# Attention kernel without softmax: the last two groups' stores go over the GpSimd queue instead of the SP queue

## The chip, the cores and the metric

The kernel runs on one core of a Trainium2 chip. A core has engines that work side by side: TensorE (PE, matrix products), VectorE (DVE), ScalarE (ACT), GpSimd (POOL) and SyncE (SP). Transfers between the device memory and the on-chip memory are done by 16 DMA engines; an instruction on an engine's queue issues a transfer and does not wait for it. The metric is the device time of one execution in microseconds (us), as the median of several runs.

## The reference

For each of 8 x 12 heads with 512 rows of 64 numbers (all float32):

```python
Q_feat = np.maximum(0, Q) + 1
K_feat = np.maximum(0, K) + 1
KV = np.einsum('bhkd,bhkv->bhdv', K_feat, V)
K_sum = np.sum(K_feat, axis=2)
numerator = np.einsum('bhqd,bhdv->bhqv', Q_feat, KV)
denominator = np.einsum('bhqd,bhd->bhq', Q_feat, K_sum)
return (numerator / (denominator[:, :, :, None] + 1e-10)).astype(np.float32)
```

Q, K, V and the output have 12.6 MB each.

## The kernel before

The rows of all heads are put into 12 groups (`NG = 12`, g = 0 to 11); a group has 1 MiB of each tensor. Two groups with the same `g // 2` share the tiles of the loads and the output tile `o_sb`, of which there are three (`OUT_BUFS = 3`).

For each group the kernel does these steps: `k_features` (L137, VectorE, maximum and addition on K), `v_blocks` (L153 and L155, V into a tile of blocks, three quarters on VectorE and one on ScalarE), `keys_values` (L171, TensorE; its result is copied by ScalarE, L181 and L182), `q_features`, `transposes` (L192, TensorE; copied at L195), `out_matmuls` (L205, TensorE) and `norms` (L222 reciprocal and L223 multiply, VectorE), which writes `o_sb`. A group has two halves h, and each half four such VectorE instructions. `store(g)` sends the group's part of `o_sb` to the output.

The order of the instructions on each engine is the order in which they are written (`tc.manual_schedule()`), and the semaphore waits between the engines follow from the data. In the main loop over g the K, V and Q loads of later groups are issued on the GpSimd queue (L106, L112), and the store of group g - 3 (`LAG = 3`) at the end of the body, on GpSimd as well. Only the very first K load goes over SP (L93). The last two groups are written out by hand after the loop; the program ends with the stores of groups 8 to 11:

```python
        output(last - 1)
        output(last)
        for g in range(last - LAG, NG):
            store(g)
```

`store` sends groups 0 to 9 over GpSimd (L126, 1 MiB each), group 10 over SP (L129, 1 MiB) and group 11 over SP in two pieces, one for each half (L132, 512 KiB each). After the last instruction the launch code (its lines in the trace are L327) closes the program: SP waits for all transfers, each engine drains (an instruction DRAIN on its queue), and the engines meet in two rounds of semaphores, in which GpSimd collects the others' signals and releases them.

Of the kernel before, what the change touches and what calls it, by code (L numbers as in the profile page):

```python
# [19 lines left out]
def kernel(  # L20
# [19 lines left out]
    nc = tc.nc  # L40
# [8 lines left out]
    NP = 4  # L49
    NG = NPAIR // NP  # L50
# [37 lines left out]
    outs = {}  # L88
# [33 lines left out]
    def store(g):  # L122
        s = g // 2
        o_to = o_dram[:, 2 * NP * s : 2 * NP * s + 2 * NP]
        if g < NG - 2:
            nc.gpsimd.dma_start(out=o_to[:, g % 2 : 2 * NP : 2], in_=outs[s][:, g % 2 : 2 * NP : 2])  # L126
            return
        if g == NG - 2:
            nc.sync.dma_start(out=o_to[:, 0 : 2 * NP : 2], in_=outs[s][:, 0 : 2 * NP : 2])  # L129
            return  # L130
        for h in range(2):
            nc.sync.dma_start(  # L132
                out=o_to[:, 2 * h + g % 2 : 2 * NP : NP], in_=outs[s][:, 2 * h + g % 2 : 2 * NP : NP]
            )

# [111 lines left out]
    with tc.manual_schedule():  # L247
# [17 lines left out]
        for g in range(last - 1):  # L265
            if g % 2:
                transposes(g - 1)
            k_features(g)
            v_blocks(g)
            if g >= 2:  # L270
                output(g - 2)
            if g % 2:
                transposes(g)
            else:
                q_features(g)
                q_features(g + 1)
            keys_values(g)
            if g % 2 and g // 2 + 2 < NG // 2:
                load_pair(g // 2 + 2)
            if g >= LAG:  # L280
                store(g - LAG)
# [5 lines left out]
        v_blocks(last)  # L287
        keys_values(last - 1)
        store(last - 1 - LAG)
        q_features(last - 1)  # L290
        q_features(last)
# [8 lines left out]
        for g in range(last - LAG, NG):  # L300
            store(g)
# [30 lines left out]
```

## Time and profile before

| | |
|---|---|
| time, median of 3 runs | 127.17 us (127.16 to 127.29) |
| span of the profiled execution, first to last instruction | 125.0 us |
| busy: VectorE, TensorE, ScalarE, GpSimd | 89.1, 62.7, 59.6, 26.1 us |
| moved by DMA queue q0 (GpSimd's) and q1 (SP's) | 28.84 and 3.15 MB |
| last multiply (L223) | 117.18 to 117.87 us |
| issues of stores 8 and 9 on GpSimd | 98.50 and 110.19 us |
| issues of store 10 and of the two pieces of store 11 on SP | 114.54, 116.22 and 117.90 us |

Apart from its span, no time of the profiled execution by itself is listed; the median lies 2.2 us above the span, which is time before the first and after the last instruction of the program. Times in the text are in us from the start of the span. POOLq and SPq are the instruction queues of GpSimd and SP: their semaphore, drain and DMA instructions stand there and don't count as busy time.

### The profile page before, as it was taken

The page shows a single profiled execution, that of the slowest core. Times are in us where ns is not written, and L with a number is a line of the kernel's source. Part 1 is how long each engine was busy: PE and PEld are TensorE (multiplying, and loading weights), DVE is VectorE, ACT ScalarE, POOL GpSimd, SP SyncE. Part 2 cuts the span into 40 slices and gives each one's busy share as a digit, 9 for nine tenths or more (in the row PEclk, how much of TensorE's full clock was granted, in tenths as well). Part 3 has the DMA queues.
Part 4 walks back from the last instruction along what each step waited for, and adds up shares of the span by engine and source line. Part 5 has one row for each costly group of instructions (what it writes and reads, how often), then busy time and mean ns, then how long its engine had stood idle before and what let it go on. Part 6 is the DMA issues. An engine that isn't in the chain of part 4 may idle for free.

```text
span 125.0 us, 2348 instructions
## 1 busy us (share of the span) xinstructions
PE 62.7 (50%) x960; PEld 51.3 (41%) x960; DVE 89.1 (71%) x190; ACT 59.6 (48%) x86; POOL 26.1 (21%) x52
## 2 busy tenths in 40 slices
PE   0004945200593837539684691079494457775300
PEld 0003735200482827428573491057393255663100
DVE  4895444206999899997999930799948699969700
ACT  7532289306029781956539462601992295450000
POOL 6991023000001630233302430302020200020000
PEclk9999999955589999995999679756999558997555
DMA  3999999999999999999999999999999999999992
GB/s 94 329 220 207 208 195 208 209 213 214 210 210 212 219 214 207 211 214 220 227 404 328 213 212 214 215 347 391 228 211 216 216 267 417 420 410 417 408 403 103
DMA packets 11803, 32.13 MB, mean 257 GB/s; under 512 B 528, under 2 KB 528, under 8 KB 11792
## 3 DMA queue, kind: packets, MB, share of 16 engines
q0 software_dynamic: 10448, 28.84, 97.2%
q1 hardware_dynamic: 1344, 3.15, 6.7%
q8 instruction: 7, 0.11, 0.3%
q14 instruction: 4, 0.03, 0.1%
HBM read 37.75 MB, written 12.58 MB: 403 GB/s over the span
## 4 chain that ended last, share of the span: by engine, by line
DMA 53%; DVE 23%; PE 8%; ACT 6%; issue 3%; POOL 2%; POOLq 0%
DMA v_raw<-in_V_dram 53%; DVE v_all L155 8%; DVE o_sb L223 8%; PE kva_ps L171 5%; ACT v_all L153 3%; DVE qf L137 2%; PE qt_ps L192 2%; DVE recip L222 2%; ACT qt L195 2%; DVE kf L137 1%; DVE qt L195 1%; ACT kva_all L181 1%; POOL v_raw L106 1%; POOL k_raw L106 1%; PE o_ps L205 1%
## 5 line engine op out<-in xcount | busy, mean ns | idle before, releaser
L205 PE MATMUL o_ps<-kva_all,qt 128*64 128x130 bf16 x384 | 20.5, 244 | 36.9 <-DVE recip L222 27.3
L171 PE MATMUL kva_ps<-v_all,kf 128*64 128x260 bf16 x384 | 30.1, 322 | 15.5 <-DVE v_all L155 15.3
L155 DVE COPY v_all<-v_raw 32x2048 bf16<-32x2048 bf16 x36 | 25.8, 717 | 13.5 <-DMA v_raw<-in_V_dram 13.1
L223 DVE TENSOR_TENSOR o_sb<-o_ps,recip 128x512 f32<-128x512 f32 x48 | 33.2, 692 | 1.7
L171 PEld LDWEIGHTS <-kf 128*64 128x64 bf16 x384 | 24.7, 131 | 18.8 <-DVE v_all L155 15.7
L205 PEld LDWEIGHTS <-qt 128*64 128x64 bf16 x384 | 14.3, 120 | 42.1 <-issue 27.3
L153 ACT COPY v_all<-v_raw 32x2048 bf16<-32x2048 bf16 x12 | 22.6, 1893 | 17.1 <-DMA v_raw<-in_V_dram 16.9
L195 ACT COPY qt<-qt_ps 128x1024 bf16<-128x1024 bf16 x23 | 22.2, 1015 | 6.7 <-PE qt_ps L192 6.4
L181 ACT CAST kva_all<-kva_ps 64x256 bf16<-64x256 f32 x24 | 8.9, 371 | 27.7 <-PE kva_ps L171 27.5
L126 POOL DMA_DIRECT2D out_dram<-o_sb x10 | 8.6, 863 | 35.9 <-DVE o_sb L223 27.5
L192 PE MATMUL qt_ps<-identity,qf 128*128 128x128 bf16 x192 | 14.9, 236 | 1.8 <-ACT qt L195 1.2
L192 PEld LDWEIGHTS <-qf 128*128 128x128 bf16 x192 | 12.5, 106 | 4.5 <-issue 2.5
L137 DVE TENSOR_SCALAR kf<-k_raw 128x1024 bf16<-128x1024 bf16 x22 | 8.5, 429 | 7.8 <-DMA k_raw<-in_K_dram 7.8
L106 POOL DMA_DIRECT2D k_raw<-in_K_dram x6 | 4.9, 811 | 35.2 <-DVE kf L137 35.2
L222 DVE RECIPROCAL recip<-o_ps 128x8 f32<-128x8 f32 x48 | 9.6, 200 | 1.4 <-PE o_ps L205 1.2
L137 DVE TENSOR_SCALAR qf<-q_raw 128x1024 bf16<-128x1024 bf16 x24 | 8.8, 432 | 2.1 <-DMA q_raw<-in_Q_dram 2.1
L106 POOL DMA_DIRECT2D v_raw<-in_V_dram x7 | 5.4, 766 | 13.1 <-ACT v_all L153 9.3
L240 DVE MEMSET v_all<- 128x2600 f32 x2 | 4.5, 2225 | 1.1 <-issue 1.1
L112 POOL DMA_DIRECT2D q_raw<-in_Q_dram x6 | 4.2, 708 | 0.0
L182 ACT CAST kva_all<-kva_ps 64x4 bf16<-64x4 f32 x24 | 4.1, 169 | 0.0
L241 ACT COPY v_all<-zero 128x1560 f32<-128x1560 f32 x2 | 2.9, 1488 | 0.0
L261 POOL MEMSET kva_all<- 128x130 bf16 x16 | 2.4, 201 | 0.0
(13 smaller groups left out, 5.7 us busy)
## 6 DMA issues: line engine op xcount, KB each, us to landing
out_dram<-o_sb POOLq DMA_DIRECT2D x10, 1024.0 KB, 25.9
q_raw<-in_Q_dram POOLq DMA_DIRECT2D x6, 1024.0 KB, 26.2
k_raw<-in_K_dram POOLq DMA_DIRECT2D x5, 1024.0 KB, 21.9
v_raw<-in_V_dram POOLq DMA_DIRECT2D x5, 1024.0 KB, 23.2
k_first<-in_K_dram SPq DMA_DIRECT2D x1, 1024.0 KB, 4.8
v_raw<-in_V_dram POOLq DMA_DIRECT2D x2, 512.0 KB, 10.7
out_dram<-o_sb SPq DMA_DIRECT2D x1, 1024.0 KB, 7.0
out_dram<-o_sb SPq DMA_DIRECT2D x2, 512.0 KB, 6.4
```

The costliest lines, as they stand in the source:

```text
L106: nc.gpsimd.dma_start(out=bufs[x, s][:, ms], in_=drams[x][:, of])
L126: nc.gpsimd.dma_start(out=o_to[:, g % 2 : 2 * NP : 2], in_=outs[s][:, g % 2 : 2 * NP : 2])
L137: nc.vector.tensor_scalar(out=dst, in0=src, scalar1=1.0, scalar2=1.0, op0=ALU.add, op1=ALU.max)
L153: nc.scalar.copy(out=v_all[ps, g % 2, :, :, b * D : b * D + D], in_=v_raw[ps])
L155: nc.vector.tensor_copy(out=v_all[ps, g % 2, :, :, b * D : b * D + D], in_=v_raw[ps])
L171: nc.tensor.matmul(kva_ps[64 * n : 64 * n + 64], lhsT=kf[:, c, n, :], rhs=v_all[:, g % 2, n, c, :], start=(c == 0), stop=(c == C2 - 1),)
L181: nc.scalar.copy(out=kva[ps, :, n, 0:D], in_=kva_ps[ps, 0 : 4 * D].rearrange("p (b d) -> p b d", b=4))
L192: nc.tensor.transpose(qt_ps[:, c, r], qf[:, r, 2 * half + c, :, :], identity)
L195: copy(out=qts[g // 2][:, lo : lo + 2], in_=qt_ps.rearrange("p c r q -> p c q r"))
L205: nc.tensor.matmul(ops[c // 4][64 * j : 64 * j + 64, c // 2 % 2, (c % 2) * W : (c % 2) * W + W], lhsT=qt[:, c, q : q + 16, :], rhs=kva[:, ...
L222: nc.vector.reciprocal(out=recip, in_=cells[:, :, :, :, D:D1])
L223: nc.vector.tensor_tensor(out=o_sb[:, 2 * h + g % 2 : 2 * NP : NP, 4 * i : 4 * i + 4].rearrange("p n (b c) d -> p b c n d", b=2), in0=cell ...
```

## The change

The stores of groups 10 and 11 are issued on the GpSimd queue, like those of all other groups: group 10 in one piece, by the branch that groups 0 to 9 take, and group 11 in the same two pieces as before. SP issues no store any more. Nothing else differs.

```diff
     def store(g):
         s = g // 2
         o_to = o_dram[:, 2 * NP * s : 2 * NP * s + 2 * NP]
-        if g < NG - 2:
+        if g < NG - 1:
             nc.gpsimd.dma_start(out=o_to[:, g % 2 : 2 * NP : 2], in_=outs[s][:, g % 2 : 2 * NP : 2])
             return
-        if g == NG - 2:
-            nc.sync.dma_start(out=o_to[:, 0 : 2 * NP : 2], in_=outs[s][:, 0 : 2 * NP : 2])
-            return
         for h in range(2):
-            nc.sync.dma_start(
+            nc.gpsimd.dma_start(
                 out=o_to[:, 2 * h + g % 2 : 2 * NP : NP], in_=outs[s][:, 2 * h + g % 2 : 2 * NP : NP]
             )
```

## The prediction

> **What bounds the kernel now.** I read the page's slices first: what limits the end?
>
> ```profile
> DMA  3999999999999999999999999999999999999992
> GB/s 94 329 220 207 208 195 208 209 213 214 210 210 212 219 214 207 211 214 220 227 404 328 213 212 214 215 347 391 228 211 216 216 267 417 420 410 417 408 403 103
> ```
>
> The 16 DMA engines are full from the second slice to the last but one; from slice 34 (103 us) on they move stores only, at 403 to 420 GB/s. Next, the windows of the last stretch (columns: window, length, busy time of PE, PEld, DVE, ACT and POOL, granted clock, DMA share, GB/s):
>
> ```profile
> 118.00:119.00 1.00, 0.00 (x0) 0.00 (x0) 0.00 (x0) 0.00 (x0) 0.00 (x0) 0.50 1.05 408
> 121.00:122.00 1.00, 0.00 (x0) 0.00 (x0) 0.00 (x0) 0.00 (x0) 0.00 (x0) 0.50 0.97 375
> 122.00:123.00 1.00, 0.00 (x0) 0.00 (x0) 0.00 (x0) 0.00 (x0) 0.00 (x0) 0.50 0.61 238
> 123.00:124.00 1.00, 0.00 (x0) 0.00 (x0) 0.00 (x0) 0.00 (x0) 0.00 (x0) 0.50 0.09 35
> ```
>
> After the last multiply (117.87 us) nothing computes; 6 us of transfers follow. The engines do not finish together: the first run dry about 122, the last at 124. Third, the DMA queues (packets, MB, time of their packets as a share of 16 engines) in the window 116 to 116.5 and then in 119 to 121; no other queue moved anything in either:
>
> ```profile
> q0 software_dynamic: 53, 0.21, 102.5%
> ```
>
> ```profile
> q1 hardware_dynamic: 419, 0.82, 105.3%
> ```
>
> q0 is POOL's queue, q1 is SP's. SP issued group 10's store at 114.54, yet up to 116.5 only q0 moves data. From 116.5 the engines change over one after the other (88.6% against 12.1% in 116 to 117, 2.1% against 105% in 118.5 to 119). So the SP stores lie behind POOL's stores 8 and 9 anyway, as if they stood in one line. Fourth, the landings: POOL's store 9 alone, then SP's last piece alone (duration, start, issue to landing):
>
> ```profile
> L126 POOL DMA_DIRECT2D out_dram<-o_sb x1: 752/752/752, 110.2 to 110.2; - x1
> ...
> DMA to landing us min/median/max: 9.1/9.1/9.1
> ```
>
> ```profile
> L132 SPq DMA_DIRECT2D out_dram<-o_sb x1: 372/372/372, 117.9 to 117.9; - x1
> ...
> DMA to landing us min/median/max: 6.2/6.2/6.2
> ```
>
> Store 9 has landed at 110.2 + 9.1 = 119.3; the last piece at 117.9 + 6.2 = 124.1. Last, what lies between that landing and the end of the span: the closing instructions of POOL, one view of 109 to 115 us and one of 124.2 to 124.35, and SP's waits:
>
> ```profile
> L327 POOLq DRAIN  x1: 10325/10325/10325, 110.2 to 110.2; - x1
> ```
>
> ```profile
> L327 POOLq EVENT_SEMAPHORE  x2: 17/17/17, 124.2 to 124.3; - x2
> ```
>
> ```profile
> SPq L327 <- DMA out_dram<-o_sb: 5.4, 4, 2.0
> ```
>
> SP waits for each store's landing, then drains; POOL's EVENT_SEMAPHORE collects the engines at 124.24, releases them, and two short drains and a second round end the span at 125.0. The row I build on is the first: POOL's closing DRAIN stands behind store 9's issue and lasts to 110.2 + 10.3 = 120.5. POOL's last issue was over at 110.9, so it is not POOL's own work that it waits out; its end lies 1.2 us behind the landing of POOL's last DMA (119.3). Now it is finished 3.7 us before anyone needs POOL.
>
> **The change part by part.**
>
> Removed: one SP issue (0.38 us) and two (0.37 us). SP has nothing else at that time; taking them away frees 0, and the transfers still wait for the same multiplies.
>
> Added: three issues on POOL, 0.75 us each as store 9 (the POOL row gives 0.75 to 1.13 for a store). The first is ready when group 10's last multiply ends (114.51), the others at 116.19 and 117.87, so POOL issues at about 114.54, 116.22 and 117.90: 1.7 us apart, each done before the next is due. Nothing else is queued on POOL between store 9 and its DRAIN.
>
> A wait that could come in: a POOL store waits for the landing of the POOL DMA eight issues before it. The waits view shows it ("POOL out_dram L126 <- DMA k_raw" 2.0 us: store 4 waited to 74.0 for the K load eight issues before). For the three new ones these are the last V load, the last Q load and store 4: landed at 99.1, 103.9 (71.32 + 32.6) and 106.5 (74.02 + 32.5). All lie before 114.5: 0.
>
> Supply: are the transfers in the queue before an engine runs dry? No row shows POOL's delay from issue to first packet on an idle queue. Bounds: 0.75 us (the issue) and 3.5 us (the first V load was issued at 1.30, its first packets come in the window 4.5 to 5.0, when the engines leave the first K load). I take 0.75, and 3.5 changes nothing: group 10's store then starts at 118.0, while the engines leave store 9 between 116.5 and 118.9; early ones idle up to 1.5 us, but they have 2 us in hand at the end (dry at 122 against 124). The last piece would be there by 121.4; the last engine gets to it at about 122.8 (landing of the piece before it, 116.2 + 6.6). The cover is this backlog; without it, up to 3.5 us less SP's own delay would stand at the end.
>
> A rule speaks against the change here. The row: store 3's issue took 1.13 us against 0.75. The Trainium skill, SBUF — State Buffer, "SBUF: two separate sides", says that GpSimd cannot write a DMA's descriptors while VectorE runs an operation in a two-port mode; its section "A bandwidth-pool intuition that's wrong (but worth ruling out)" gives 620 ns growing to about 3100. No issue here is that long; by 3.1 us the last piece would be queued at 121.0, still ahead of 122.8, and the sum would stay.
>
> Pace: 2 MB move from q1 to q0. q0 alone moves 417 GB/s in 106 to 110, q1 alone 409 in 119 to 121: 5.03 against 5.13 us for 2.1 MB, a gain of 0.1 us at best. By landings, stores 5 to 8 landed at 109.0, 111.5, 114.0 and 116.5 (79.3 + 29.7 up to 98.5 + 18.0), 2.5 us per MB; 3 MB more from 116.5 give 124.0 to 124.1, which is where SP's last piece lands now. So I take 0, and keep -0.1. The last landing stays at 124.1.
>
> The close: POOL's DRAIN now stands behind the issue at 117.9. If it follows the last POOL landing as it does now, it ends at 124.1 + 1.2 = 125.3, and POOL's EVENT_SEMAPHORE moves from 124.24 to 125.33 (0.03 us behind the drain, as behind the later drain at 124.41 + 0.10). SP's waits end as now, so POOL is the last to arrive. Cost 1.1 us. Everything after it (125.0 - 124.24 = 0.7 us) moves along: span 126.1. Bounds of the 1.2 us: it is one reading; at 0.2 us the cost would be 0.1, at 1.9 (half as much again) 1.7.
>
> Here a second rule differs from the trace. The row: 10.3 us of DRAIN, 9.6 of them after POOL's issue had ended. The Trainium skill, PSUM — Partial Sum Buffer, "Engine vs sequencer instructions", says that a drain waits until the engine is fully idle and speaks of no transfers; read so, the drain would end with the last issue, about 118.7, and the change would cost 0. The row decides.
>
> Sum: 0 (SP) + 0 (POOL's issues) + 0 (supply) + 0 (pace) + 1.1 (drain). The profiled execution has a span of 125.0 us; the median of the three runs is 127.17, so 2.2 us lie outside the span and stay. 125.0 + 1.1 + 2.2 = 128.3; from the median, 127.17 + 1.09 = 128.26.
>
> **The rivals.**
>
> No cost (not slower): the drain has no tie to the landing, or its 1.2 us shrink when the queue empties. Then the end is the last landing as now: 127.07 to 127.2. It decides from the point where the drain ends less than 0.4 us after the landing (0.17 brings it to 124.24, 0.25 more is the bound of what can be told). For it: one reading only. Against: POOL had no work in these 9.6 us, and of the events nearby only store 9's landing comes close before the end.
>
> A fixed drain: it lasts 9.6 us behind POOL's last issue whatever the transfers do. Last issue over at 118.65, drain to 128.2, event 4.0 us later than now: 131.2. Against: three other drains of POOL, with no transfer open, last 0.05 to 0.2 us.
>
> A starved tail: POOL's issues are slow beside VectorE, or its queue starts later than 3.5 us, and engines run dry for 0.5 to 1.5 us besides the drain: 128.8 to 129.8. The rows against it are those of the supply.
>
> **How the numbers follow.** Drain behind the landing 0.80 (127.7 to 128.9), no cost 0.10, fixed drain 0.03, starved tail 0.04, a gain of more than 0.25 us for a reason I don't see 0.03. A difference under 0.2% (0.25 us) can't be told from none: slower 0.87, same 0.10, faster 0.03. Range 127.5 to 129.0: it leaves out no cost, fixed drain, the unseen gain and most of the starved tail, together 0.19.
>
> **What would show it.** The profile after should have a POOL DRAIN from 117.9 to about 125.3, ending 1.2 us behind the last landing; that landing at 124.1; no q1 packets after the first K load; and POOL's event right behind its drain, with SP waiting for it. A last landing off 124.1 by over 0.3 us breaks supply or pace; a drain ending by 124.2 breaks the forecast.

## The result, and the profile after

The changed kernel takes 128.28 us (median of 6 runs, 127.73 to 128.44) where the kernel before took 126.98 us in the same series (6 runs, 126.41 to 127.29): a ratio of 1.0103, with an interval of 1.0078 to 1.0128. The change costs 1.3 us. (The six runs before include the three that the prediction started from, 127.16 to 127.29; the three new ones took 126.41 to 126.80.) The profiled execution took 128.1 us, with a span of 126.3 us against 125.0 before.

Line numbers behind `store` are three lower in the changed kernel: the multiply is L220, and the closing instructions are L324. First the transfers of the tail, in the page's slices (now 3.16 us each) and in the queues between 120 and 122 us (packets, MB, share of 16 engines):

```profile
DMA  3999999999999999999999999999999999999980
GB/s 80 331 220 206 210 191 211 212 217 215 207 211 212 219 212 210 209 213 217 261 412 281 208 213 215 218 384 359 217 210 219 215 323 416 422 412 412 414 348 9
```

```profile
q0 software_dynamic: 221, 0.82, 100.2%
```

The stores move through q0 alone and at the same pace (412 to 422 GB/s in the full slices; 0.82 MB in these 2 us, as q1 had in its two). What is new is the last slice: 9 GB/s where there had been 103. The program goes on after its transfers are over. The last piece's issue and landing, POOL's closing drain with the event behind it (a window around 125.6), and SP's waits show why:

```profile
L129 POOL DMA_DIRECT2D out_dram<-o_sb x1: 719/719/719, 118.9 to 118.9; - x1
...
DMA to landing us min/median/max: 5.3/5.3/5.3
```

```profile
L324 POOLq DRAIN  x1: 6722/6722/6722, 118.9 to 118.9; - x1
L324 POOLq EVENT_SEMAPHORE  x1: 17/17/17, 125.6 to 125.6; - x1
```

```profile
SPq L324 <- DMA out_dram<-o_sb: 122.9, 5, 115.6
SPq L324 <- PEq L324: 1.8, 2, 1.3
```

The last piece has landed at 118.88 + 5.3 = 124.2. The drain lasts to 118.86 + 6.72 = 125.58, and only then, at 125.62, does POOL collect the engines. Before, that event stood at 124.24. The last wait of SP, 1.3 us, is new. Before, it was 0.5 us:

```profile
SPq L327 <- PEq L327: 0.6, 2, 0.5
```

In the view after, the wait is put down to PE's queue, but PE had drained by 117.7; what came last was POOL's drain. A releaser's name in such a line is a guess that the times have to confirm.

### The profile page after: what moved, and what is told of

Its sections match the earlier page's. It is cut to its first block, busy times and chain, and to the rows that moved or that the text cites. A ratio compares the mean times of both kernels' runs of the same rounds, so it can differ in the third digit from the quotient of the medians.

```text
span 126.3 us, 2349 instructions
## 1 busy us (share of the span) xinstructions
PE 66.7 (53%) x960; PEld 53.9 (43%) x960; DVE 89.6 (71%) x190; ACT 59.6 (47%) x86; POOL 28.4 (22%) x55
## 3 DMA queue, kind: packets, MB, share of 16 engines
q0 software_dynamic: 11008, 30.94, 100.3%
## 4 chain that ended last, share of the span: by engine, by line
DMA 52%; issue 24%; POOL 6%; DVE 5%; ACT 4%; PE 3%; POOLq 1%
DMA v_raw<-in_V_dram 30%; DMA out_dram<-o_sb 22%; DVE v_all L152 3%; PE kva_ps L168 2%; POOL out_dram L126 2%; ACT qt L192 2%; ACT v_all L150 2%; POOL v_raw L106 1%; DVE o_sb L220 1%; POOL q_raw L112 1%; POOLq L324 1%; ACT kva_all L178 1%; POOL k_raw L106 1%; POOL out_dram L129 1%; PE o_ps L202 1%
## 5 line engine op out<-in xcount | busy, mean ns | idle before, releaser
L168 PE MATMUL kva_ps<-v_all,kf 128*64 128x260 bf16 x384 | 35.2, 359 | 14.8 <-DVE v_all L152 14.8
L202 PE MATMUL o_ps<-kva_all,qt 128*64 128x130 bf16 x384 | 20.0, 240 | 35.3 <-DVE recip L219 24.3
L168 PEld LDWEIGHTS <-kf 128*64 128x64 bf16 x384 | 28.0, 148 | 19.6 <-DVE v_all L152 15.2
L220 DVE TENSOR_TENSOR o_sb<-o_ps,recip 128x512 f32<-128x512 f32 x48 | 33.2, 692 | 1.7
L126 POOL DMA_DIRECT2D out_dram<-o_sb x11 | 9.4, 853 | 39.2 <-DVE o_sb L220 27.8
```

The lines of the kernel that those rows point to most:

```text
L168: nc.tensor.matmul(kva_ps[64 * n : 64 * n + 64], lhsT=kf[:, c, n, :], rhs=v_all[:, g % 2, n, c, :], start=(c == 0), stop=(c == C2 - 1),)
L202: nc.tensor.matmul(ops[c // 4][64 * j : 64 * j + 64, c // 2 % 2, (c % 2) * W : (c % 2) * W + W], lhsT=qt[:, c, q : q + 16, :], rhs=kva[:, ...
L220: nc.vector.tensor_tensor(out=o_sb[:, 2 * h + g % 2 : 2 * NP : NP, 4 * i : 4 * i + 4].rearrange("p n (b c) d -> p b c n d", b=2), in0=cell ...
```

## The experiments

Two theories stood at the start. **A:** POOL's closing DRAIN ends a certain distance behind the landing of POOL's own last DMA, and only what of that reaches beyond SP's last wait costs time. **B:** every byte that is moved from SP's queue to POOL's costs something by itself, through late supply or a slower pace. A third, **C**, was that any move away from SP costs. Four kernels put the three issues on different queues. (The experiments' kernels choose the queue in a variable, so their line numbers are off by one or a few: the closing instructions are L324 to L328, the issues of the last pieces L129 to L133.)

**The first two on POOL, the last piece on SP.** Against the changed kernel:

```diff
-        for h in range(2):
-            nc.gpsimd.dma_start(
+        for h, queue in enumerate((nc.gpsimd, nc.sync)):
+            queue.dma_start(
```

> Store 10 and the first piece of store 11 on POOL, the last piece on SP. Theory A (the closing drain of POOL ends 1.2 to 1.35 us behind the landing of POOL's own last DMA, and costs only what of that lies behind SP's last wait): POOL's last landing about 122.9, drain to 124.1 to 124.3, SP's last landing 124.1; the close is where it was, cost 0 to 0.1 us, time within 0.2% of before. Theory B (the 1.5 MB of 2 MB moved to POOL cost by themselves, through supply or pace): about three quarters of the change's 1.3 us, so +1.0 us.

Measured: ratio 1.0035 (1.0016 to 1.0055), +0.44 us. The interval, 0.2 to 0.7 us, holds neither A's 0 to 0.1 nor B's 1.0. The profile says why:

```profile
L130 POOL DMA_DIRECT2D out_dram<-o_sb x1: 707/707/707, 116.6 to 116.6; - x1
...
DMA to landing us min/median/max: 6.8/6.8/6.8
```

```profile
L325 POOLq DRAIN  x1: 8097/8097/8097, 116.6 to 116.6; - x1
```

POOL's last piece lands at 123.3 and not at 122.9, because SP's piece, issued at 118.0, is served beside it: SP's first packet starts at 119.30, POOL's last one at 122.93. Behind store 10's last landing (121.62) the last landings of the two pieces follow 1.72 and 0.80 us apart, where in the changed kernel they follow 1.25 apart. The drain ends 1.31 us behind that landing, at 124.65, and POOL's event comes 0.56 us behind the last of all landings, against 0.17 before. The difference, 0.39 us, lies within the interval of the cost. The theory's distance was right; the landing that I had put into it was wrong.

**Only store 10 on POOL.** Against the kernel before:

```diff
-        if g < NG - 2:
+        if g < NG - 1:
...
-        if g == NG - 2:
-            nc.sync.dma_start(out=o_to[:, 0 : 2 * NP : 2], in_=outs[s][:, 0 : 2 * NP : 2])
-            return
```

> Only store 10 on POOL, both pieces of store 11 on SP. Theory A: POOL's last landing about 121.6, drain to 122.9, over 1.2 us before SP's last landing of 124.1: cost 0. Theory B: half of the 2 MB is moved, +0.65 us.

Measured: ratio 0.9998 (0.9974 to 1.0021). Half of the bytes are moved and nothing is lost; B's +0.65 us is out.

```profile
L325 POOLq DRAIN  x1: 8661/8661/8661, 115.3 to 115.3; - x1
```

POOL's drain lasts from 115.34 to 124.00, behind a landing at 122.73, and is over 0.6 us before the last landing (124.62 in this execution). I had expected a margin of 1.2 us; as in the first experiment, SP's pieces are served beside POOL's store, which lands 3.15 us behind store 9 and not 2.5.

**Only the last piece on POOL.** Against the kernel before:

```diff
-        for h in range(2):
-            nc.sync.dma_start(
+        for h, queue in enumerate((nc.sync, nc.gpsimd)):
+            queue.dma_start(
```

> Store 10 and the first piece of store 11 on SP as before, only the last piece (512 KiB) on POOL. Theory A: POOL's last landing about 124.1, drain to 125.3 to 125.4, the whole cost of the change: +1.1 to +1.35 us. Theory B: a quarter of the 2 MB is moved, +0.3 us.

Measured: ratio 1.0106 (1.0083 to 1.0129), +1.3 us: the whole cost of the change with a quarter of its bytes.

```profile
L130 POOL DMA_DIRECT2D out_dram<-o_sb x1: 707/707/707, 118.0 to 118.0; - x1
...
DMA to landing us min/median/max: 6.1/6.1/6.1
```

```profile
L325 POOLq DRAIN  x1: 7411/7411/7411, 117.9 to 117.9; - x1
```

Landed at 124.09, drained at 125.36. It is the landing of POOL's last DMA that counts, not how many bytes were moved.

**All three on ScalarE's queue** (`nc.scalar` where the kernel before has `nc.sync` in `store`).

> All three issues on the ScalarE queue instead of SP's. Theory A: what matters is that POOL's queue is not the last to finish, so as before: POOL's drain ends 1.2 us behind store 9's landing, about 120.5, and the time is within 0.3% of before. Theory C (any move off SP costs, because SP's queue is the quickest to start or to close): +0.5 us or more.

Measured: ratio 1.0010 (0.9993 to 1.0026). The interval ends at +0.33 us, so C, which asks for 0.5 us or more, is out.

```profile
L325 POOLq DRAIN  x1: 10338/10338/10338, 110.4 to 110.4; - x1
```

POOL's drain ends at 120.69, as before the change, long before anyone asks.

**How far behind?** The distance was not one number: 1.231 us before the change (29 DMAs issued by POOL), 1.271 in the second and third experiment (30), 1.311 in the first (31), 1.353 after the change (32). The next kernels vary the size of the last DMA and the number of DMAs.

**64 KiB of the last piece on POOL.** Against the kernel before:

```diff
-        for h in range(2):
-            nc.sync.dma_start(
-                out=o_to[:, 2 * h + g % 2 : 2 * NP : NP], in_=outs[s][:, 2 * h + g % 2 : 2 * NP : NP]
-            )
+        nc.sync.dma_start(out=o_to[:, 1 : 2 * NP : NP], in_=outs[s][:, 1 : 2 * NP : NP])
+        nc.sync.dma_start(out=o_to[:, 3 : 2 * NP : NP, 0:7], in_=outs[s][:, 3 : 2 * NP : NP, 0:7])
+        nc.gpsimd.dma_start(out=o_to[:, 3 : 2 * NP : NP, 7:8], in_=outs[s][:, 3 : 2 * NP : NP, 7:8])
```

> As before the change, except that of the last piece (512 KiB) the last 256 bytes of each 2 KiB row, 64 KiB in all, go over POOL; the rest stays on SP. Theory A (the drain ends behind the landing of POOL's last DMA, however small that is, by 42.4 ns for each DMA that POOL has issued, here 30): POOL's last landing about 124.1, drain 1.27 us behind it, cost +1.1 to +1.3 us. Theory B (cost by moved bytes): 64 KiB of 2 MiB, +0.04 us.

Measured: ratio 1.0041 (1.0027 to 1.0055), +0.5 us, which is neither figure.

```profile
L131 POOL DMA_DIRECT2D out_dram<-o_sb x1: 706/706/706, 118.4 to 118.4; - x1
...
DMA to landing us min/median/max: 5.4/5.4/5.4
```

```profile
L324 POOLq DRAIN  x1: 6696/6696/6696, 118.3 to 118.3; - x1
```

POOL's small piece did not come last: it landed at 123.77, SP's at 124.34. The drain ended 1.272 us behind POOL's landing, at 125.04, so the distance is what A says, and POOL's event is 0.58 us later than SP alone would allow, which agrees with the cost measured. Three percent of the moved bytes still cost about ten times what B allows.

**Stores 5 to 9 in four pieces each, 47 DMAs on POOL.** Against the changed kernel, where this loop replaces the first branch's single issue:

```diff
+            step = 2 if 5 <= g < NG - 2 else 2 * NP
+            for n in range(0, 2 * NP, step):
+                nc.gpsimd.dma_start(
+                    out=o_to[:, n + g % 2 : n + step : 2], in_=outs[s][:, n + g % 2 : n + step : 2]
+                )
```

> As the changed kernel, and the stores of groups 5 to 9 are issued on POOL in four pieces of 256 KiB each, so that POOL issues 47 DMAs instead of 32. Theory A1 (the distance from POOL's last landing to the end of its drain is 42.4 ns for each DMA issued): 1.99 us. Theory A2 (the distance is fixed, or goes with the few DMAs still open when the drain begins; the 1.23 to 1.35 us seen so far are scatter): 1.2 to 1.4 us. The time by A1, with the last landing unchanged: 0.6 us above the changed kernel, about +1.9 us against before; by A2 +1.3 us.

```profile
L133 POOL DMA_DIRECT2D out_dram<-o_sb x1: 719/719/719, 118.2 to 118.2; - x1
...
DMA to landing us min/median/max: 5.9/5.9/5.9
```

```profile
L328 POOLq DRAIN  x1: 7897/7897/7897, 118.2 to 118.2; - x1
```

The last landing is the usual one, 124.15; the drain ends at 126.12, 1.966 us behind it. The time is 1.0173 of before (1.0150 to 1.0195), +2.2 us. A1 (a count) had put the distance at 1.99, A2 (fixed) at 1.2 to 1.4: it goes with the number of DMAs. It is not the bytes, since POOL's queue moves 30.94 MB here as in the changed kernel.

**All stores on SP but the last piece, and all stores on SP.** The diffs only replace `nc.gpsimd` by `nc.sync` in `store`.

> All stores on SP except the last piece of 512 KiB, which is on POOL: POOL issues 20 DMAs (19 loads and this one). Theory A1: the drain ends 20 x 42.4 ns = 0.85 us behind the landing of the last piece. Theory A2: 1.2 to 1.4 us. The time is no clean test, since the stores no longer stand behind the loads in one queue; the distance is.

> All stores on SP, POOL issues the 19 loads only. Theory A1: POOL's drain is over 19 x 42.4 ns = 0.81 us behind the landing of the last load, far ahead of the close, so nothing is gained or lost there against before. What the stores do beside the loads is open: they may start before loads that they now wait behind (the loads then land later, the computation with them), time -1 to +3 us.

Measured: distances of 0.863 us with 20 DMAs and 0.823 us with 19, where A1 had 0.85 and 0.81. With 19 the drain lasts from 82.54 to 117.54, behind the last load's landing at 116.72:

```profile
L324 POOLq DRAIN  x1: 34999/34999/34999, 82.5 to 82.5; - x1
```

The times are 1.0941 (1.0913 to 1.0970) and 1.0824 (1.0810 to 1.0838) of before. The +8.2% is outside my -1 to +3 us. In that kernel the last Q load lands at 116.7 us (103.9 before the change), and the last stores find the engines half empty (its page):

```profile
GB/s 97 317 218 208 212 204 210 211 219 207 213 226 267 260 246 260 264 268 269 262 251 249 223 261 268 249 251 252 249 261 267 259 249 270 337 31 185 127 400 220
```

From slice 13 to 34 the rate stays at 223 to 270 GB/s, where before the change stretches near 210 alternated with slices of 330 to 400: stores and loads now go side by side (in 40 to 48 us, 144 GB/s in POOL's queue and 115 in SP's, against 212 and 0 before), and the loads, which the computation waits for, come later: VectorE's waits for V loads grow from 13.1 to 24.3 us in all. The kernel with the stores behind the loads in one queue is 10 us faster; that the later loads are the whole of it is argued, not shown.

**A second drain before store 10**, in the changed kernel:

```diff
         for g in range(last - LAG, NG):
+            if g == NG - 2:
+                nc.gpsimd.drain()
             store(g)
```

> The changed kernel with one more DRAIN on POOL between the issues of store 9 and store 10. So far the distance from POOL's last landing to the end of its closing drain is 0.05 us and 41 ns for each DMA that POOL has issued (19, 20, 29 to 32 and 47 of them). The new drain should end 0.05 + 29 x 0.041 = 1.24 us behind store 9's landing, about 120.5, and then stores 10 and 11 are issued one behind the other into a queue that has run dry. Theory P (a drain clears away the DMAs issued since the last drain): the closing drain then ends 0.05 + 3 x 0.041 = 0.17 us behind the last landing. Theory Q (it goes through all DMAs since the start each time): 1.36 us. In both the run is slower than the changed kernel, by about 2 to 4 us, and the gap between the issue of store 10 and its first packet shows POOL's start on an idle queue, which the prediction bounded by 0.75 and 3.5 us.

One run: 130.5 us, beside 126.93 of the kernel before. The added drain, then the closing one:

```profile
L299 POOLq DRAIN  x1: 10068/10068/10068, 110.1 to 110.1; - x1
```

```profile
L326 POOLq DRAIN  x1: 6175/6175/6175, 121.8 to 121.8; - x1
```

The first ends at 120.20, 1.230 us behind store 9's landing (118.97). The second ends at 127.96, 0.165 us behind the last landing (127.79): three DMAs, not 32. Theory P had 0.17, Q 1.36; P holds.

All distances from the landing of POOL's last DMA to the end of the drain behind it, from the traces' event times:

| kernel | DMAs issued by POOL since the drain before | distance, us | 0.048 us + 40.8 ns each |
|---|---|---|---|
| second drain (closing) | 3 | 0.165 | 0.170 |
| all stores on SP | 19 | 0.823 | 0.823 |
| all but the last piece on SP | 20 | 0.863 | 0.864 |
| before; ScalarE's queue; second drain (first) | 29 | 1.230 to 1.231 | 1.231 |
| store 10; last piece; 64 KiB on POOL | 30 | 1.271 to 1.272 | 1.272 |
| the first two on POOL | 31 | 1.311 | 1.313 |
| after | 32 | 1.353 | 1.354 |
| stores 5 to 9 in pieces | 47 | 1.966 | 1.966 |

The line is fitted through 19 and 47; the other rows test it, to 5 ns. What POOL does in those 41 ns per DMA isn't seen in any row, and why most of it comes behind the last landing, although the older DMAs had landed long before, stays open.

## Why the prediction was right, point by point

**Direction and size.** 128.26 was forecast and 128.28 measured; that they agree so closely is luck, because two errors cancel. The kernel before took 126.98 us in the series of the result (126.72 in the 29 runs beside the first four experiments), less than the 127.17 that the sum started from, and the step was +1.3 us instead of +1.1. The same shows in the parts: the span became 126.3 and not 126.1, and the 2.2 us that the sum put outside the span are 1.7 to 1.8 in every listed run of both kernels. The 2.2 came from a median of three runs less the span of one profiled execution. In the span the whole difference is at POOL's event, 125.62 against the 125.33 of the sum: 0.15 us of it is the drain, 0.13 the landing, 0.01 the step from the drain to the event.

**The drain: mechanism right, size short by 0.15 us.** The term of 1.2 us (1.231 in the trace) was read as a constant, with bounds of 0.2 and 1.9 (by the sum's own terms the upper one costs 1.8 us, not 1.7). It is a count: three more DMAs add 3 x 41 ns = 0.12 us, and it became 1.353. One reading could not show that; the range covered it.

**The landing: 124.2 instead of 124.1.** In the kernels here that end with SP's or ScalarE's stores, the one with all stores on SP aside, the last landing lay between 124.07 and 124.62, so this is within the scatter of single executions.

**POOL's issues: about 1 us later than forecast, at no cost.** They were put where SP's had been, at 114.54, 116.22 and 117.90; they came at 115.52, 117.20 and 118.88. The multiplies themselves ended 0.71 us later in this execution. The rest was overlooked: POOL's issue starts 0.29 us behind the multiply that it waits for, SP's 0.03. The rows before the change have it (store 9 was issued at 110.19, its last multiply ended at 109.90). The transfers still ahead in the queue covered all of it.

**Supply.** Right, though the 0.75 us taken for it was too little. On an idle queue, in the second drain's kernel, store 10 is issued at 120.78 and its first packet starts at 122.11: 1.3 us, between the bounds of 0.75 and 3.5. In the changed kernel the first of store 10's 16 landings, one for each engine, is 2.74 us behind the first of store 9's, not 2.50: the earliest engine loses 0.24 us. The last landing is 2.49 us behind, so the last engine, which sets the end, loses none. The rule of the Trainium skill, SBUF — State Buffer, "SBUF: two separate sides", had spoken against the change here. The three issues took 0.71 to 0.75 us, the first two beside the multiplies and the third after them, and no starving shows.

**Pace and the wait for eight DMAs back.** Both 0, as put. On the last engine store 10 lands 2.49 us behind store 9, and the two pieces 1.25 us behind one another: the 2.5 us per MB of before.

**One line.** That SP's stores "stand as if in one line" behind POOL's was too strong. It holds for the handover before the change, but in the first two experiments SP's pieces were served beside POOL's and made them land 0.5 and 0.65 us later.

**The rivals.** "No cost" is excluded by the time, and by the drain's end in every kernel here. "A fixed drain" is excluded by its end 6.0 us behind POOL's last issue, where it had been 9.6 before. "A starved tail" fell with supply. The rule of the Trainium skill, PSUM — Partial Sum Buffer, "Engine vs sequencer instructions", that a drain waits for the engine to go fully idle, says too little for POOL: here its drain waits for the landing of the transfers that it has issued (in the kernel with all stores on SP for 34 us behind the last issue), and some time for each of them.

No version that beats the kernel before came out. There POOL's drain is over 3.7 us before it is needed, so fewer DMAs on POOL would gain nothing at the end.

## What to carry to other kernels

Look at what closes a program, not only at its last transfer: in this one GpSimd's drain waits for GpSimd's own transfers and then takes 41 ns for each DMA issued there, so the last transfer belongs on SP's or ScalarE's queue, and GpSimd's last one should land about 0.05 us + 41 ns per DMA earlier. A long DRAIN in the trace that starts with the last issue and covers nothing now is a cost that waits for a change to uncover it. When one distance is read from one profile, ask what it might be a count of, and bound it so. And take the time outside the span from one and the same execution: the 2.2 us here were 1.8.

## What the runs showed of the hardware that was not expected

The drain's distance is a count of DMAs since the drain before (40.8 ns each and 0.05 us, from 3 to 47 DMAs). GpSimd's issue of a store starts 0.29 us behind the multiply that it waits for, SP's and ScalarE's 0.03 us. A transfer from GpSimd into an idle queue had its first packet 1.3 us after the start of its issue. Between SP's and GpSimd's queues the order in which pieces land is not that of issue: 64 KiB from GpSimd, issued last, landed 0.57 us before SP's last piece, and 512 KiB from SP delayed GpSimd's piece by about 0.5 us.
